# One decoder step on one core: an MLP seam without GpSimd, other PSUM banks for two transposes per head pair, and decode transposes later

## The chip, the cores and the metric

The kernel runs on one core of one Trainium2 chip. The metric is the device time of one execution in microseconds, the median of several runs. The core has a TensorE (PE) for matmuls, VectorE (DVE), ScalarE (ACT) and GpSimd (POOL) for elementwise work, SyncE (SP), which here only issues DMAs, and 16 DMA engines. Each engine works through its own instruction list in order and waits on semaphores of the others. Matmul results land in PSUM, which the kernel uses as eight banks; everything else lives in SBUF.

## The reference

One layer of a hybrid decoder, for 512 new tokens of one sequence (prompt) and one new token for each of 8 sequences with a window of 2048 cached rows (sample). All numbers are fp32.

```python
D_MODEL = 2048; SEQ = 512; DEC_BATCH = 8; DEC_SEQ = 1; PAST_LEN = 4096
HEAD_DIM = 64; N_HEADS = 16; D_FF = 4 * D_MODEL; D_IN = 3 * 1024 + 3 * 1024
DILATED_CONFIGS = ((128, 1), (512, 4), (2048, 16))

def reference(...):
        q, k, v, u, gb = _mixer_inputs(xp, norm_mix[l], w_in[l], q_norm[l], k_norm[l])
        o = _combine_branches([_dilated_branch_prompt(q, k, v, bias_c, d)
                               for bias_c, (_, d) in zip(biases, DILATED_CONFIGS)])
        ...
        yc = _depthwise_conv(ucat, conv_w[l], s_p)
        xp = xp + _mixer_output(o, yc, gb, attn_out_norm[l], conv_out_norm[l], w_out[l])
        xp = xp + _mlp(xp, norm_mlp[l], w_up[l], w_down[l])
        ...
        q, k, v, u, gb = _mixer_inputs(xs, norm_mix[l], w_in[l], q_norm[l], k_norm[l])
        kcat = jnp.concatenate([state_attn_k[l].astype(k.dtype), k], axis=1)
        ...
        ks_new.append(kcat[:, t_s:t_s + wb])      # the state shifted by one row
        vs_new.append(vcat[:, t_s:t_s + wb])

def _mlp(x, g, w_up, w_down):
    h = _rmsnorm(x, g)
    a = jnp.square(jax.nn.relu(jnp.einsum('bsd,df->bsf', h, w_up)))
    return jnp.einsum('bsf,fd->bsd', a, w_down)
```

The outputs are both token streams, the new keys and values of the prompt, and for the samples the key and value states of 8 x 2048 rows shifted by one row, which is a copy of some 131 MB from memory to memory (read and written).

## The kernel before

**Matmuls in three passes.** An fp32 operand is split into a high part `whi` (a rounded copy, on ScalarE) and a low part `wlo` (the rest, a subtraction on VectorE; L148/L149 for projections, L787/L788 in the MLP). A product is then three passes: high by high, high by low, low by high, on tiles of 128 rows by 260 columns (512 prompt and 8 sample tokens make two such halves). A weight tile of 512 KB is loaded by SyncE, split, and used by one product.

**Attention stage** (to about 420 us). `proj` runs the projections of q, k and v for eight head pairs j = 0..7 through `block` (L213). Inside a product, `step` is called after every third matmul and lets a generator advance: `norm_gen` (the RMS norm of q and k, its matmul on L408) and `attn_gen` (the attention of a pair). A `yield from wait(n)` means n such steps, so 3n matmuls. The order of instructions on each engine is fixed by the order in which this code emits them. `attn_gen` emits for each pair: scores of four row blocks into the `pS` banks (two heads, two banks), their softmax, then transposes. `trans(hp, tb)` (L475) transposes the normalized weights of head `hp` and row block `tb` on TensorE (L479), and evicts them as a high part on ScalarE (L482) and a low part on VectorE (L483). `pv(hp)` (L485) multiplies them by the values into a `pS` bank (L489). For a pair the order is trans(0,0) to trans(0,2) among the scores, trans(0,3), `pv(0)`, trans(1,0) to trans(1,3), `pv(1)`. PSUM is handed out in turn: `wtile` (L204) gives one of two `pw` banks, `stile` (L207) one of two `pS` banks. An instruction that writes a bank waits until the bank's previous readers are done.

**Decode stage** (about 420 to 690 us). The conv projections run on TensorE, and `dec_gen` (L561) advances beside them in the same way. It computes the 8 samples' attention: VectorE multiplies keys by queries, the scores are transposed, normalized (L635, L636), transposed again on L641, and the values of each batch b = 0..7 are multiplied, added (L664, L669) and summed with a matmul on L674. Batch b's wait ahead of L674 is 10 steps.

**MLP** (about 860 to 2166 us). 64 groups of seven products each (Winograd's form of a 2 x 2 block product, product number n = 7 gi + pi): groups 0 to 31 are the up half, groups 32 to 63 the down half in eight chunks c of four. A product is 24 matmuls of L1030, and after two of three of them `step` is called. `q_prep(n)` loads the four weight quarters of the next group (`q_load`, tiles `rg` and `raw`), splits the operand of product n + 2, and does one of the four sums of quarters that Winograd's form needs (`q_sum`, L848): sum 1 of the next group at pi = 3, sum 2 at pi = 5, sum 3 at pi = 0, sum 4 at pi = 1. Two things are special. In groups below `ADDED` = 4, sum 1 is done by a DMA that GpSimd issues and that adds the fourth quarter to the second while it loads (L826, L828). And `on_vector(gi, i)` (L837) gives sums 2 and 4 of group 31 and sums 1, 2 and 4 of group 32 to GpSimd instead of VectorE.

At the seam (groups 30 to 32) the down half's operands of chunk 0 must be ready: `op_gen(0)` loads and splits seven operands (`put`, L1001: two ScalarE and two VectorE instructions on L787/L788, tile `R`), one in each product of group 31.

**State shift.** `copy_chunk` (L135) issues one of 368 copies of 356 KB from SyncE. In the MLP two of three products issue one (L1100).

Of the kernel before, what the change touches and what calls it, by code (L numbers as in the profile page):

```python
# [33 lines left out]
NB = 8  # L34
# [50 lines left out]
def hymba_kernel(ctx, tc, xT, wi, wo, wu, wd, state_k, state_v, sconv, relb, relrep, ohp, lcp, ohd, lcd,  # L85
# [111 lines left out]
    def wait(n):  # L197
        for _ in range(n):
            yield
# [4 lines left out]
    def wtile():  # L204
        return p2.tile([128, 512], F32, name="pw", bufs=2)

    def stile():  # L207
        return p2.tile([128, 512], F32, name="pS", bufs=2)
# [216 lines left out]
    def attn_gen(j):  # L425
        while done.get(("norm", j)) != 2:
            yield
        if j not in TB:
            load_T(j)
        yield from wait(1 if j else 10)  # L430
        st = wtile()
        for i in range(3):
            T.transpose(st[:NB, i * 128:(i + 1) * 128], flat(RAW[i, j])[:, SEQ:], ident)
        yield from wait(3)
        stg = wt((NB, 3, 128), name="stg")
        S.activation(stg.rearrange("p a b -> p (a b)"), st[:NB, :384], AF.Copy)
        SP.dma_start(scr_qkv[:, :, j * 128:(j + 1) * 128], stg)
        st = wtile()
        for s in range(4):
            T.transpose(st[:, s * 128:(s + 1) * 128], flat(RAW[2, j])[:, s * 128:(s + 1) * 128], ident)  # L440
        yield from wait(3)
        sv = st.rearrange("p (s h e) -> p h s e", s=4, h=2)
        S.activation(vv[:, :, :, 0], sv, AF.Copy)
        V.tensor_tensor(vv[:, :, :, 1], sv, vv[:, :, :, 0].bitcast(F32), OP.subtract)
        yield
        pt = {}

        def products(tb):

            w = (tb + 1) * 128  # L450
            q = slice(tb * 128, (tb + 1) * 128)
            ss = [stile() for _ in range(2)]
            for n, (a, b) in enumerate(((qh, kh), (qh, kl), (ql, kh))):
                for hp in range(2):
                    r = slice(hp * E, (hp + 1) * E)
                    T.matmul(ss[hp][:, :w], a[r, q], b[r, :w], start=n == 0, stop=n == 2)
            return ss

        def score(hp, tb, s):
            w = (tb + 1) * 128  # L460
            lg = late(j, tb) if hp else wt((128, 512), name="lg")
            sm = wk.tile([128, 4], F32, name="sm", bufs=8)
            V.tensor_tensor_reduce(out=lg[:, :w], in0=s[:, :w], in1=TB[j][:, hp, 512 - w:], scale=1.0, scalar=-3e38,
                                   op0=OP.add, op1=OP.max, accum_out=sm[:, 0:1])
            V.tensor_scalar(sm[:, 1:2], sm[:, 0:1], -1.0, None, op0=OP.mult)
            S.activation(lg[:, :w], lg[:, :w], AF.Exp, bias=sm[:, 1:2], accum_out=sm[:, 2:3])
            pt[hp, tb] = lg, sm

        def norm_p(hp, tb):
            w = (tb + 1) * 128  # L470
            lg, sm = pt[hp, tb]
            V.reciprocal(sm[:, 3:4], sm[:, 2:3])
            V.tensor_scalar(lg[:, :w], lg[:, :w], sm[:, 3:4], None, op0=OP.mult)

        def trans(hp, tb):  # L475
            lg, sm = pt.pop((hp, tb))
            st = wtile()
            for s in range(tb + 1):
                T.transpose(st[:, s * 128:(s + 1) * 128], lg[:, s * 128:(s + 1) * 128], ident)  # L479
            sv = st.rearrange("p (s t) -> p s t", s=4)[:, :tb + 1]  # L480
            q = slice(tb * 128, (tb + 1) * 128)
            S.activation(pth[:, :tb + 1, q], sv, AF.Copy)  # L482
            V.tensor_tensor(ptl[:, :tb + 1, q], sv, pth[:, :tb + 1, q].bitcast(F32), OP.subtract)  # L483

        def pv(hp):  # L485
            st = stile()
            for s in range(4):
                for n, b in enumerate((pth, ptl)):
                    T.matmul(st[:, s * 128:], vv[:, hp, s].rearrange("p c e -> p (c e)"), b[:, s, s * 128:],  # L489
                             start=s == 0 and n == 0, stop=s == 3 and n == 1, skip_group_check=True)  # L490
                yield
            r = slice(hp * E, (hp + 1) * E)
            o = flat(R3[:, j])[r, :SEQ]
            S.activation(o, st[:E, :], AF.Copy)
            V.tensor_tensor(o, st[E:, :], o, OP.add)
            yield

        for tb in range(4):
            ss = products(tb)
            for hp in range(2):  # L500
                score(hp, tb, ss[hp])
            yield from wait(4)
            if tb == 3:
                done["scores"] = j + 1
            for hp in range(2):
                norm_p(hp, tb)
            yield from wait(4)
            if tb:
                trans(0, tb - 1)
            yield from wait(3)  # L510
        if j < 6:
            toeplitz(j + 2)
        trans(0, 3)
        yield from wait(5)
        yield from pv(0)
        for tb in range(4):
            trans(1, tb)
            yield from wait(4)
        yield from wait(2)
        yield from pv(1)  # L520
# [40 lines left out]
    def dec_gen():  # L561
# [72 lines left out]
        yield from wait(2)  # L634
        V.reciprocal(sm[:, 3:4], sm[:, 2:3])  # L635
        V.tensor_scalar(lg, lg, sm[:, 3:4], None, op0=OP.mult)  # L636
        yield from wait(2)
        yield from wait(2)
        st = wtile()
        for g in range(3):  # L640
            T.transpose(st[:NP[g], g * 128:(g + 1) * 128], lg[:, GOFF[g]:GOFF[g] + NP[g]], ident)  # L641
# [17 lines left out]
        for n in range(len(items) + 1):  # L659
            if n < len(items):  # L660
                b, g = items[n]
                t = tiles["v", b, g]
                w = pT[:NP[g], g, b * H:(b + 1) * H]
                V.tensor_tensor(t[:NP[g]], t[:NP[g]], w[:, :, None].to_broadcast([NP[g], H, E]), OP.mult)  # L664
            yield from wait(6)
            if n and items[n - 1][1]:
                b, g = items[n - 1]
                a = tiles["v", b, 0]
                V.tensor_tensor(a[:NP[g]], a[:NP[g]], tiles.pop(("v", b, g))[:NP[g]], OP.add)  # L669
                if g == 2:  # L670
                    a = tiles.pop(("v", b, 0)).rearrange("p h e -> p (h e)")
                    yield from wait(10)
                    for c in range(4):
                        T.matmul(od[32 * c:32 * c + 32, :256], sel[:, 31 - b:63 - b], a[:, 256 * c:256 * c + 256],  # L674
                                 start=b == 0, stop=b == NB - 1, skip_group_check=True)
                    prev(n + 2)
            prev(n + 2)
            yield from wait(3)
# [121 lines left out]
                                          for o in range(2) for h in range(2)}))  # L800
    NG = len(groups)
    Q = {}
    ADDED = 4

    def q_load(gi, o, h):
        if gi >= NG:
            return
        src = groups[gi][3][o, h]
        if o == 0:
            t = sl.tile([128, 8, 128], F32, name="raw", bufs=3)  # L810
            Q[gi, o, h] = t
            SP.dma_start(t, src)
        elif gi < 2:
            Q[gi, o, h] = [wt((128, 4, 128), name="rw") for _ in range(2)]
            for i in range(2):
                SP.dma_start(Q[gi, o, h][i], src[:, 4 * i:4 * i + 4])
        else:
            t = gt([128, 8, 128], name="rg")
            Q[gi, o, h] = t
            SP.dma_start(t, src)  # L820
        if (o, h) == (1, 0) and gi < ADDED:

            a22 = groups[gi][3][1, 1]
            if gi < 2:
                for i in range(2):
                    P.dma_start(Q[gi, o, h][i], a22[:, 4 * i:4 * i + 4], accum_op=OP.add)  # L826
            else:
                P.dma_start(t, a22, accum_op=OP.add)  # L828
# [5 lines left out]
        else:  # L834
            yield qs

    def on_vector(gi, i):  # L837

        if gi < 31:
            return True  # L840
        return i in {31: (1, 3), 32: (3,)}.get(gi, (1, 2, 3, 4))

    def q_sum(gi, i):
        out, a, b, op = SUMS[i]
        if gi < NG and not (i == 1 and gi < ADDED):
            e = V if on_vector(gi, i) else P
            for o_, a_, b_ in pieces(Q[gi, *out], Q[gi, *a], Q[gi, *b]):
                e.tensor_tensor(o_, a_, b_, op)  # L848

    SUMS = {1: ((1, 0), (1, 0), (1, 1), OP.add),  # L850
            2: ((0, 0), (1, 0), (0, 0), OP.subtract),
# [233 lines left out]
    for n in range(7 * NG):  # L1085
# [11 lines left out]
            C_ = pa.tile([128, 2, 512], F32, name=nm[pa], bufs=2)  # L1097
        ps = {0: A_, 1: None if pi < 1 else D_, 3: None if pi < 3 else C_}[{0: 0, 1: 1, 2: 0, 3: 3, 4: 0, 5: 1, 6: 0}[pi]]
        q_prep(n)
        if n % 3 != 2:  # L1100
            copy_chunk()
        product(n, ps, op_view(XO[OPS[pi]] if kind == "up" else DO[c, OPS[pi]]), 8 if kind == "up" else 4)

# [62 lines left out]
        if kind == "up" and gi == 31:  # L1166
# [3 lines left out]
                free_slots.extend(dslots[2 * pi - 4:2 * pi - 2])  # L1170
            if pi == 0:
                gens[0] = op_gen(0)
            next(gens[0])
        elif kind == "down":
            if g == 3:
                free_slots.append(DO.pop((c, OPS[pi])))
            if c == 0 and (g, pi) in ((0, 0), (1, 0)):
                free_slots.append([[wk.tile([128, 2, HT], F32R, name="wo", tag="w", bufs=16)
                                    for _ in range(2)] for _ in range(2)])
# [81 lines left out]
```

## Time and profile before

| | us |
|---|---|
| median of 3 runs | 2166.95 (2166.39 to 2168.46) |
| the profiled execution | 2167.66 |
| its span, first to last instruction | 2166.0 |
| TensorE busy | 2134.5 (99%) |
| VectorE busy | 1766.3 (82%) |
| ScalarE busy | 957.9 (44%) |
| GpSimd busy | 68.5 (3%) |
| DMA | 459.83 MB in 137935 packets |

Busy times come from one profiled execution. A matmul's length in the profile overlaps the next one's, so TensorE counts as busy as long as matmuls follow each other without a pause. Where it is not busy, the profile names the instruction on another engine whose end released it. All times in the text count from the span's start.

### The profile page before, as it was taken

How to read it: one execution, taken by the hardware profiler on the slowest of the kernel's cores; microseconds unless marked ns; L12 is line 12 of the kernel's file. 1: busy time of each engine (PE TensorE's matmuls, PEld its weight loads, DVE VectorE, ACT ScalarE, POOL GpSimd, SP SyncE). 2: the span in 40 equal slices, each digit the busy share in tenths (PEclk: the TensorE clock that was granted, in tenths of full speed). 3: DMA queues.
4: the chain of work that ended last, by engine and by line, in shares of the span. 5: the costliest groups of instructions: out<-in, count | busy, mean ns of one | idle time of the engine just before them, and what ended most of it. 6: DMA issues, size and time to landing. Idle time of an engine off the chain costs nothing.

```text
span 2166.0 us, 42326 instructions
## 1 busy us (share of the span) xinstructions
PE 2134.5 (99%) x17594; PEld 2105.7 (97%) x17594; DVE 1766.3 (82%) x2421; ACT 957.9 (44%) x1379; POOL 68.5 (3%) x83
## 2 busy tenths in 40 slices
PE   8999999999999999999999999999999999999999
PEld 8888999999999999999999999999999999999999
DVE  7777776698786657798888888888999999999997
ACT  5444444321223235554444444445444444444443
POOL 1001010000000000000000000002000000000000
PEclk9999999999999999999999999999999999999999
DMA  5344543476464647666776676677876666666653
GB/s 208 124 165 148 169 161 113 139 229 210 153 186 155 245 155 243 226 221 241 253 236 219 245 246 215 246 253 269 314 291 250 225 226 251 231 224 246 239 200 122
DMA packets 137935, 459.83 MB, mean 212 GB/s; under 512 B 19504, under 2 KB 49840, under 8 KB 131344
## 3 DMA queue, kind: packets, MB, share of 16 engines
q1 hardware_dynamic: 136320, 454.81, 60.4%
q0 software_dynamic: 864, 2.10, 0.5%
q8 instruction: 138, 2.26, 0.4%
q14 instruction: 53, 0.43, 0.1%
q10 hardware_dynamic: 560, 0.22, 0.0%
HBM read 414.31 MB, written 181.16 MB: 275 GB/s over the span
## 4 chain that ended last, share of the span: by engine, by line
PE 63%; DVE 4%; ACT 1%; issue 1%; DMA 1%; DVEq 0%; SPq 0%
PE mn L1030 29%; PE mm L1030 29%; PE mm L213 5%; DVE R L788 1%; DVE wlo L149 1%; DVE wlo L788 1%; DVE x1t L934 0%; DVE acc L927 0%; DMA ra<-scr_a 0%; ACT sq L925 0%; ACT whi L148 0%; ACT x L936 0%; ACT R L936 0%; ACT R L787 0%; DMA ovs<-state_v 0%
## 5 line engine op out<-in xcount | busy, mean ns | idle before, releaser
L213 PE MATMUL mm<-R,whi 128*128 128x260 f32 x4000 | 677.7, 287 | 5.7 <-ACT whi L148 5.6
L213 PEld LDWEIGHTS mm<-R,whi 128*128 128x128 f32 x4000 | 560.8, 189 | 19.0 <-issue 8.6
L1030 PE MATMUL mm<-R,whi 128*128 128x260 f32 x3008 | 547.7, 283 | 1.7 <-ACT cs L1113 1.2
L1030 PE MATMUL mn<-R,whi 128*128 128x260 f32 x3008 | 547.5, 283 | 0.0
L1030 PEld LDWEIGHTS mm<-R,whi 128*128 128x128 f32 x3008 | 463.3, 188 | 2.1 <-ACT cs L1113 1.4
L1030 PEld LDWEIGHTS mn<-R,whi 128*128 128x128 f32 x3008 | 463.3, 188 | 0.1
L1030 PE MATMUL mn<-R,wlo 128*128 128x260 f32 x1504 | 425.0, 283 | 2.4 <-DVE wlo L788 2.4
L1030 PE MATMUL mm<-R,wlo 128*128 128x260 f32 x1504 | 425.1, 283 | 1.3 <-DVE wlo L788 1.3
L213 PE MATMUL mm<-R,wlo 128*128 128x260 f32 x2000 | 404.0, 284 | 0.0
L788 DVE TENSOR_TENSOR wlo<-raw,whi 128x1024 fp32r<-128x1024 f32 x255 | 311.9, 1223 | 109.3 <-ACT whi L787 107.5
L787 ACT ACTIVATE whi<-raw 128x1024 fp32r<-128x1024 f32 x255 | 269.3, 1056 | 207.4 <-PE mn L1030 95.3
L213 PEld LDWEIGHTS mm<-R,wlo 128*128 128x128 f32 x2000 | 310.0, 189 | 0.4
L787 ACT ACTIVATE whi<-rg 128x1024 fp32r<-128x1024 f32 x186 | 197.3, 1061 | 215.9 <-PE mn L1030 91.5
L1030 PEld LDWEIGHTS mn<-R,wlo 128*128 128x128 f32 x1504 | 283.2, 188 | 3.0 <-DVE wlo L788 3.0
L1030 PEld LDWEIGHTS mm<-R,wlo 128*128 128x128 f32 x1504 | 283.2, 188 | 1.8 <-DVE wlo L788 1.7
L788 DVE TENSOR_TENSOR wlo<-rg,whi 128x1024 fp32r<-128x1024 f32 x186 | 228.1, 1226 | 1.5 <-ACT whi L787 1.4
L148 ACT ACTIVATE whi<-raw 128x1024 fp32r<-128x1024 f32 (+1 forms) x129 | 133.7, 1038 | 167.5 <-PE mm L213 134.0
L149 DVE TENSOR_TENSOR wlo<-raw,whi 128x1024 fp32r<-128x1024 f32 (+1 forms) x129 | 155.5, 1206 | 45.6 <-ACT whi L148 43.6
L848 DVE TENSOR_TENSOR raw<-raw 128x1024 f32<-128x1024 f32 x62 | 75.6, 1219 | 0.0
L848 DVE TENSOR_TENSOR rg<-rg,raw 128x1024 f32<-128x1024 f32 x62 | 75.5, 1218 | 0.0
L848 DVE TENSOR_TENSOR raw<-rg,raw 128x1024 f32<-128x1024 f32 x60 | 73.5, 1225 | 2.1
L1150 DVE TENSOR_TENSOR yacc<-mm,yacc 128x520 f32<-128x520 f32 x96 | 66.6, 694 | 7.3 <-PE mm L1030 6.3
(227 smaller groups left out, 2291.2 us busy)
## 6 DMA issues: line engine op xcount, KB each, us to landing
oks<-state_k SPq DMA_DIRECT2D x184, 356.0 KB
ovs<-state_v SPq DMA_DIRECT2D x184, 356.0 KB
raw<-wi SPq DMA_DIRECT2D x94, 512.0 KB
raw<-wu SPq DMA_DIRECT2D x64, 512.0 KB
rg<-wd SPq DMA_DIRECT2D x64, 512.0 KB
raw<-wd SPq DMA_DIRECT2D x64, 512.0 KB
rg<-wu SPq DMA_DIRECT2D x60, 512.0 KB
raw<-wo SPq DMA_DIRECT2D x32, 512.0 KB
```

Of the source, the lines that this page charges most:

```text
L148: S.activation(his[i][:, h], raws[i][:, h], AF.Copy)
L149: V.tensor_tensor(los[i][:, h], raws[i][:, h], his[i][:, h].bitcast(F32), OP.subtract)
L213: T.matmul(ps[t][:, :HT] if isinstance(ps, tuple) else ps[:, t, :HT], a[:, k, :], b[:, t, :], start=start and n == 0, stop=stop and n == 2)
L787: S.activation(hi, src, AF.Copy)
L788: eng.tensor_tensor(lo, src, hi.bitcast(F32), OP.subtract)
L848: e.tensor_tensor(o_, a_, b_, op)
L1030: T.matmul(ps[:, r, :HT], a[:, k, :], b(kt), start=n % 7 in ((0, 1, 3) if kts == 8 else (0, 1)) and kt == 0 and m == 0, stop=kt == kts - 1 ...
L1150: V.tensor_tensor(dst[:, r], v[:, r], dst[:, r], OP.add)
```

## The change

Five edits. Line numbers behind them differ by up to seven.

- In `trans`, blocks (0,3) and (1,0) of each pair take a bank with `stile` (`pS`) and not with `wtile` (`pw`).
- In `dec_gen`, the transposes of the normalized scores come 9 steps after the normalization, where it was 4, and the last batch waits 14 steps ahead of L674, where it was 10.
- `on_vector` is gone: no Winograd sum runs on GpSimd. Sum 1 of groups 31, 32 and 33 is done by the accumulating load that groups 0 to 3 have; the other sums of these groups run on VectorE.
- `copy_chunk` is not called in groups 30 to 32, and is called in every product of groups 4 to 10.
- `op_gen(0)` advances at pi = 0, 2, 4, 6 of group 31 and pi = 0, 2, 3 of group 32, where it was every product of group 31.

```diff
         def trans(hp, tb):
             lg, sm = pt.pop((hp, tb))
-            st = wtile()
+
+            st = stile() if (hp, tb) in ((0, 3), (1, 0)) else wtile()
...
         V.tensor_scalar(lg, lg, sm[:, 3:4], None, op0=OP.mult)
-        yield from wait(2)
-        yield from wait(2)
+        yield from wait(9)
         st = wtile()
...
-                    yield from wait(10)
+                    yield from wait(10 if b < NB - 1 else 14)
...
-    ADDED = 4
+    ADDED = (0, 1, 2, 3, 31, 32, 33)
...
-        if (o, h) == (1, 0) and gi < ADDED:
+        if (o, h) == (1, 0) and gi in ADDED:
...
-    def on_vector(gi, i):
-
-        if gi < 31:
-            return True
-        return i in {31: (1, 3), 32: (3,)}.get(gi, (1, 2, 3, 4))
-
     def q_sum(gi, i):
         out, a, b, op = SUMS[i]
-        if gi < NG and not (i == 1 and gi < ADDED):
-            e = V if on_vector(gi, i) else P
+        if gi < NG and not (i == 1 and gi in ADDED):
             for o_, a_, b_ in pieces(Q[gi, *out], Q[gi, *a], Q[gi, *b]):
-                e.tensor_tensor(o_, a_, b_, op)
+                V.tensor_tensor(o_, a_, b_, op)
...
-        if n % 3 != 2:
+        if not 30 <= gi <= 32 and (n % 3 != 2 or 4 <= gi <= 10):
             copy_chunk()
...
-            next(gens[0])
+            if pi % 2 == 0:
+                next(gens[0])
...
+            if gi == 32 and pi in (0, 2, 3):
+                next(gens[0])
```

TensorE's order in pair 0, around transposes (0,3) and `pv(0)`, before (`mm` is a projection's bank, `ident` the identity that a transpose multiplies by):

```order
L213 MATMUL mm<-R_76,whi 128x260 x3
L408 MATMUL pw<-sq,bd 128x260 x2
L479 MATMUL pw<-ident,lg 128x128 x4
L213 MATMUL mm<-R_76,whi 128x260
L213 MATMUL mm<-R_76,wlo 128x260 x2
L213 MATMUL mm<-R_76,whi 128x260 x4
L213 MATMUL mm<-R_76,wlo 128x260 x2
```

The same place after the change:

```order
L213 MATMUL mm<-R_76,whi 128x260 x3
L408 MATMUL pw<-sq,bd 128x260 x2
L480 MATMUL pS<-ident,lg 128x128 x4
L213 MATMUL mm<-R_76,whi 128x260
L213 MATMUL mm<-R_76,wlo 128x260 x2
L213 MATMUL mm<-R_76,whi 128x260 x4
L213 MATMUL mm<-R_76,wlo 128x260 x2
```

No instruction has moved; the four transposes write another bank.

VectorE's order at the seam before, from the end of group 30 into group 31 (`R` is an operand split of `put`, `wlo` a weight split, `cs` an eviction):

```order
L788 TENSOR_TENSOR wlo<-raw,whi 128x1024
L848 TENSOR_TENSOR rg<-rg,raw 128x1024
L788 TENSOR_TENSOR R_76<-ra,R_76 128x520 x2
L788 TENSOR_TENSOR wlo<-raw,whi 128x1024
L788 TENSOR_TENSOR R_76<-ra,R_76 128x520 x2
L788 TENSOR_TENSOR wlo<-rg,whi 128x1024
L788 TENSOR_TENSOR R_76<-ra,R_76 128x520 x2
L788 TENSOR_TENSOR wlo<-raw,whi 128x1024
L1115 TENSOR_TENSOR cs<-mn,cs 128x260
L788 TENSOR_TENSOR R_76<-ra,R_76 128x520 x2
L788 TENSOR_TENSOR wlo<-rg,whi 128x1024
L1117 TENSOR_TENSOR cs<-mn,cs 128x260
```

The same place after the change (L841 is the sum that was L848, L1108, L1110 and L1112 the evictions that were L1115, L1117 and L1119):

```order
L788 TENSOR_TENSOR wlo<-raw,whi 128x1024
L841 TENSOR_TENSOR rg<-rg,raw 128x1024
L788 TENSOR_TENSOR R_76<-ra,R_76 128x520 x2
L788 TENSOR_TENSOR wlo<-raw,whi 128x1024
L841 TENSOR_TENSOR raw<-raw 128x1024
L788 TENSOR_TENSOR wlo<-rg,whi 128x1024
L788 TENSOR_TENSOR R_76<-ra,R_76 128x520 x2
L788 TENSOR_TENSOR wlo<-raw,whi 128x1024
L1108 TENSOR_TENSOR cs<-mn,cs 128x260
L788 TENSOR_TENSOR wlo<-rg,whi 128x1024
L1110 TENSOR_TENSOR cs<-mn,cs 128x260
L788 TENSOR_TENSOR R_76<-ra,R_76 128x520 x2
```

Every second pair of `R` splits has moved back, and sum 4 of group 31, which GpSimd did, stands where one of them was.

GpSimd's last instructions before, from its accumulating loads on:

```order
L826 DMA rw<-wu 128x512 x4
L828 DMA rg<-wu 128x1024 x2
L848 TENSOR_TENSOR raw<-rg,raw 128x1024
L848 TENSOR_TENSOR raw<-raw 128x1024
L848 TENSOR_TENSOR rg<-rg 128x1024
L848 TENSOR_TENSOR raw<-rg,raw 128x1024
L848 TENSOR_TENSOR raw<-raw 128x1024
```

And after the change:

```order
L715 COPY cs_o<-up 128x8
L826 DMA rw<-wu 128x512 x4
L828 DMA rg<-wu 128x1024 x3
L828 DMA rg<-wd 128x1024 x2
L1248 UNCONDITIONAL_BRANCH
```

The five sums are gone, and three accumulating loads of groups 31 to 33 have come.

## Rows read from the trace of the kernel before

**Rows 1.** Windows by stage: busy us per engine, granted clock, DMA share, GB/s.

```profile
core 0: us, PE busy (x) PEld busy (x) DVE busy (x) ACT busy (x) POOL busy (x), PEclk, DMA share, GB/s
...
860.00:900.00 40.00, 36.18 (x295) 35.31 (x294) 35.31 (x52) 25.77 (x44) 2.62 (x3) 1.00 0.80 262
900.00:1480.00 580.00, 580.00 (x4833) 579.88 (x4831) 485.68 (x581) 278.25 (x380) 0.86 (x1) 1.00 0.68 233
...
1500.00:1532.00 32.00, 28.68 (x230) 27.66 (x229) 31.97 (x34) 17.86 (x26) 9.06 (x3) 1.00 1.00 370
...
1550.00:1600.00 50.00, 50.00 (x419) 50.00 (x418) 48.36 (x57) 23.06 (x25) 0.00 (x0) 1.00 0.93 351
```

**Rows 2.** TensorE's waits, whole span: us in total, times, longest.

```profile
PE pw L479 <- DVE R L483: 9.1, 11, 1.3
...
PE pw L674 <- DVE kv L669: 1.0, 1, 1.0
PE pw L641 <- DVE lg L636: 0.9, 1, 0.9
```

**Rows 3.** TensorE's waits from 1450 to 1560 us, the seam.

```profile
PE mn L1030 <- DVE wlo L788: 1.7, 2, 1.5
PE mm L1030 <- DVE wlo L788: 0.9, 1, 0.9
PE mm L1030 <- DVE yacc L1150: 0.5, 1, 0.5
PE mn L1030 <- ACT R L787: 0.2, 1, 0.2
```

**Rows 4.** The page's costliest groups: busy us, mean ns of one, idle before.

```profile
L1030 PE MATMUL mm<-R,whi 128*128 128x260 f32 x3008 | 547.7, 283 | 1.7 <-ACT cs L1113 1.2
```

**Rows 5.** Timeline of VectorE in pair 1: start, us, instruction.

```profile
131.91 0.55 DVE L483 TENSOR_TENSOR R<-pw,R 128x384 fp32r<-128x384 f32 x1
132.37 1.21 DVE L149 TENSOR_TENSOR wlo<-raw,whi 128x1024 fp32r<-128x1024 f32 x1
```

**Rows 6.** Timeline of TensorE, pairs 0 and 1: start, us, instruction, idle before.

```profile
87.82 0.66 PE L479 MATMUL pw<-ident,lg 128*128 128x128 f32 x4 [1.16 <-DVE R L483]
...
90.12 0.62 PE L489 MATMUL pS<-R 128*128 128x512 f32 x2
...
130.84 0.50 PE L408 MATMUL pw<-sq,bd 128*128 128x260 f32 x2 [0.86 <-DVE h L414]
132.51 1.10 PE L479 MATMUL pw<-ident,lg 128*128 128x128 f32 x4 [1.16 <-DVE R L483]
...
136.36 0.63 PE L489 MATMUL pS<-R 128*128 128x512 f32 x2
...
146.06 0.65 PE L479 MATMUL pw<-ident,lg 128*128 128x128 f32 x4 [0.81 <-DVE R L483]
```

**Rows 7.** A window in pair 1, columns as in rows 1.

```profile
133.00:134.00 1.00, 1.00 (x6) 1.00 (x5) 0.59 (x1) 0.35 (x1) 0.00 (x0) 0.50 0.00 0
```

**Rows 8.** Timeline of GpSimd at the seam, three of its five sums.

```profile
1488.60 2.43 POOL L848 TENSOR_TENSOR raw<-rg,raw 128x1024 f32<-128x1024 f32 x1 [586.33 <-DVE wlo L788]
...
1502.28 3.41 POOL L848 TENSOR_TENSOR rg<-rg 128x1024 f32<-128x1024 f32 x1 [2.88 <-DMA rg<-wd]
...
1523.06 3.25 POOL L848 TENSOR_TENSOR raw<-raw 128x1024 f32<-128x1024 f32 x1 [7.15 <-DVE rg L848]
```

**Rows 9.** Timeline of VectorE at the seam.

```profile
1489.66 1.93 DVE L1130 SCALAR_TENSOR_TENSOR cs<-cs,rstd 128x520 f32<-128x520 f32 x1
...
1492.99 0.69 DVE L1130 SCALAR_TENSOR_TENSOR cs<-cs,rstd 128x520 f32<-128x520 f32 x1
...
1495.11 1.22 DVE L848 TENSOR_TENSOR rg<-rg,raw 128x1024 f32<-128x1024 f32 x1
...
1513.31 0.41 DVE L1119 TENSOR_TENSOR cs<-mm,cs 128x260 f32<-128x260 f32 x1
...
1524.59 2.81 DVE L788 TENSOR_TENSOR wlo<-rg,whi 128x1024 fp32r<-128x1024 f32 x1
```

**Rows 10.** Line 828, the accumulating loads of groups 2 and 3.

```profile
DMA to landing us min/median/max: 6.4/7.5/8.7
```

## The prediction

> **What bounds the kernel now.** I read the stages first, then what TensorE waits for, then the lines around each wait. In most of the program TensorE is never idle: in groups 2 to 29 of the MLP it is busy 580.00 of 580 us [rows 1], so nothing outside TensorE's own idle time can be won. The list of its waits over the whole span shows where that idle time is: 9.1 us in 11 waits of the transposes on line 479, each for VectorE's L483, and one wait each of 0.9 and 1.0 us in the decode stage, at L641 and L674 [rows 2]. The list for 1450 to 1560 us adds the MLP seam, where the up products end and the down products begin: 1.7 + 0.9 + 0.5 + 0.2 = 3.3 us in five waits [rows 3]. There VectorE is the bound: 31.97 us busy in 32, with TensorE at 28.68 [rows 1].
>
> A wait costs a little more than the idle time listed. A 260-column matmul is modelled 283 ns long [rows 4], but matmuls follow each other every 580.00/4833 = 0.120 us [rows 1], so each wait also loses 0.283 - 0.120 = 0.16 us of overlap. I add 0.16 per removed wait.
>
> **Attention: two transposes on score banks.** The waits on L479 come from the bank, not from the data. Before transposes (0,3) of pair j = 1, L483 reads the previous result out of a bank at 131.91 for 0.55 us, so until 132.46 [rows 5]; the transposes start at 132.51, after 1.16 us of idle time [rows 6]. There are two `pw` banks, the norm's L408 takes one of them in between, and so the transposes need the bank that L483 has not yet emptied. In the change, transposes (0,3) and (1,0) go to the `pS` banks, which are free there: the scores of the pair are long evicted, and `pv(0)` takes the other one. The order of work on TensorE is the same; only the bank differs. With (1,0) out of the `pw` turn, (1,1) and (1,2) also find a bank whose last reader is long done. One of the 11 waits stays, (1,3) of pair 1 at 146.06 with 0.81 us [rows 6], because (1,2) and (1,3) still share a turn. So 9.1 - 0.81 = 8.3 us in ten waits, plus 10 x 0.16, is 9.9 us. L408's wait of 0.86 us [rows 6] is for L414, which the change does not touch; I leave it.
>
> There is more at pair 1. From the start of transposes (0,3) to the start of `pv(0)` the same instructions take 90.12 - 87.82 = 2.30 us in pair 0 and 136.36 - 132.51 = 3.85 us in pair 1 [rows 6]. [...]
>
> One new wait is to be paid. With (0,3) of pair 1 starting 1.3 us earlier, `pv(0)` is due at 132.51 - 1.32 + 2.30 = 133.49, but the low part of its operand (L483) stands on VectorE behind the L149 that ends at 132.37 + 1.21 = 133.58 [rows 5]; 0.69 us of L483 behind that puts the second matmul of `pv(0)` about 0.5 us late. Attention: 9.9 + 1.55 - 0.5 = **10.9 us**. Bounds: 6 if half of the waits return at the next bank, 11.5 if the new wait does not come.
>
> **Decode.** L641's transposes move 5 steps later; a step is three matmuls, so 15 x 0.12 = 1.8 us against the 0.9 us they waited. The last batch's L674 moves 4 further steps, 1.44 us against 1.0. Both waits go: 0.9 + 1.0 + 2 x 0.16 = 2.2 us. The whole V phase moves 5 steps later against the projections, whose VectorE work keeps its place. So the additions L669 of batches 0 and 2 land behind other VectorE instructions, the largest of which is a split of 1.21 us like L149 [rows 5]. By the order a wait of about 0.3 us appears at each; bounds 0 and 1.2 each. Nothing else is queued behind on TensorE but projections. The key and value loads that SyncE issues from these steps pass one or two weight loads, which have whole products of lead; the phase still ends before the projections do. I cost that at nothing, and at up to 1 us if the lead were gone. Decode: 2.2 - 0.6 = **1.6 us** (0.5 to 2.2).
>
> **The seam.** Before, GpSimd does five of the Winograd sums between 1488.60 and 1526.3, 2.4 to 3.4 us each [rows 8]. Beside each one a VectorE instruction is stretched: L1130 takes 1.93 us at 1489.66 and 0.69 at 1492.99; the last of five is a split at 1524.59 with 2.81 instead of 1.21 [rows 9]. Together the five lose 9.3 us. With GpSimd idle this is gone. VectorE gets four of the five sums at 1.22 us each [rows 9] and loses two that it had, as sum 1 of groups 31, 32 and 33 becomes an accumulating load: +2.4 us. Three of seven operand splits move from group 31 into group 32; each is two VectorE instructions on 128x520 tiles like L1130 at 0.69 us [rows 9], so 4.1 us of work moves to where its due times are later. Net: VectorE has 6.9 us less to do in a stretch in which TensorE lost 3.3 + 5 x 0.16 = 4.1 us to it. By the new order it stays within 0.1 to 1 us of each due time, so I leave 0.4 us of waits. Seam: **3.7 us**, bounds 4.1 and -2 (lower if a sum stands in front of a split that is due).
>
> The accumulating loads must land before sum 2 reads them, or VectorE stops in order, with the splits behind it, and TensorE behind those. In the first seam two such loads landed 6.4 to 8.7 us after their issue [rows 10]. For group 32, both plain loads had landed by 1502.28, when GpSimd's third sum started [rows 8]; the first of the two, which is all that the accumulate needs, is issued ahead, and without the copies in the queue it should be there by about 1499. Then 1499 + 7.5 to 8.7 is 1506.5 to 1508; sum 2 is now in the row ahead of the eviction that ran at 1513.31 in the slowed order of before [rows 9], and TensorE had lost some 2 us by then. That is 2 to 4 us of room; the other groups have about the same. I cost the loads at nothing; without that room each microsecond of lateness is one of VectorE.
>
> [...]
>
> The copies: 16 more in groups 4 to 10 and 14 fewer in groups 30 to 32. The DMA share is 0.68 in 900 to 1480 [rows 1]; a 356 KB copy occupies the engines for about 1 us, so 16 of them in seven groups of 20 us are 16/141 = 0.11 more, some 0.8. At a share of 0.93, TensorE is still busy 50.00 us of 50 [rows 1]. Cost: nothing; at most 16 x 1 us if every copy delayed a weight load that was due.
>
> **Sum.** 10.9 + 1.6 + 3.7 = 16.2 us. The profiled execution took 2167.66 us, its span 2166.0; 2167.66 - 16.2 = 2151.5. The median of the runs is 0.7 us lower, so 2150.8; I say 2151.
>
> **Rivals.** First, VectorE keeps the clock of attention: the removed waits come back at the next instruction that needs it, as at `pv(0)` of pair 1. For it: the remaining waits on L414 and L483 [rows 6]. Against it: most pairs have only one or two short waits, with matmuls of a projection between. If half returns, attention gives 5.5 and not 10.9: 2156.5.
>
> Second, the clock falls in pair 1 all the same, since the wait of 0.86 us stays: 1.55 us less, 2152.5.
>
> Third, the slower side: the accumulating loads starve at the seam. VectorE has about 6.9 - 4.1 = 2.8 us to spare there, so a total lateness of L costs L - 2.8. With landing 12 us after issue each load is about 2.5 us late, 7.5 in all: 4.7 lost, 2155.7. To end slower than before by over 0.2%, L must be 16.2 + 4.3 + 2.8 = 23 us, about 7.8 per load, so landing some 17.5 us after issue, twice the longest row [rows 10]; at 20 us it would be 2151 + 31.5 - 2.8 = 2180.
>
> Fourth, the denser copies saturate the queues in groups 4 to 10: by their own length at most 16 us, which ends at about 2167, no change.
>
> Fifth, the change does not do what it says: the transposes wait at the `pS` banks as they did at `pw`. Then only decode and seam are left: 2166.95 - 5.3 = 2161.6.
>
> **How the numbers follow.** Forecast 0.68 (2147 to 2154, the low end if the waits at 130.84 and 146.06 shrink too); first rival 0.10; second 0.07; third 0.07, of which 0.03 slower; fourth 0.05, of which 0.02 faster, 0.02 no change and 0.01 slower; fifth 0.03, at the edge of no change. A measurement of this kernel tells about 0.2%, 4.3 us, from no change. Faster: 0.68 + 0.10 + 0.07 + 0.04 + 0.02 = 0.91; the same 0.05; slower 0.04. The range of 2147.5 to 2159 takes in the forecast, the first two rivals and the milder side of the third.
>
> **What would show it.** Right: no wait on the transposes' line but one of 0.8 us near 140 us; granted clock 1.00 throughout attention; no wait at the decode transposes; L1130 and the splits at the seam at 0.69 and 1.21 us, TensorE busy 31.5 of 32 us there; the new loads landing within 9 us. Wrong: waits on L483 moved to `pv`, a long VectorE wait on a DMA in groups 31 to 33, or TensorE waiting for splits in groups 4 to 10.

## The result and the profile after

The changed kernel takes 2150.82 us (median of 4 runs, 2150.38 to 2151.33) beside 2167.16 us for the kernel before (4 runs, 2166.39 to 2168.46): a ratio of 0.9924, with a 95% interval from 0.9912 to 0.9936. The prediction was 2151.0. Its profiled execution took 2150.38 us with a span of 2148.4.

TensorE's waits over the whole span of the changed kernel (us in total, times, longest us; L480 is the transposes' line, L479 before, and L490 the weighted sum, L489 before), against [rows 2]:

```profile
PE pw L408 <- DVE h L414: 1.5, 3, 0.9
...
PE pw L480 <- DVE R L484: 0.8, 1, 0.8
...
PE pS L490 <- DVE R L484: 0.7, 2, 0.4
...
PE pw L674 <- DVE kv L669: 0.3, 1, 0.3
```

Of 9.1 us in 11 waits of the transposes one of 0.8 us is left; L641 is gone from the list, and L674 keeps 0.3 of 1.0 us. From 1450 to 1560 us, against [rows 3]:

```profile
PE mn L1023 <- DVE yacc L1143: 0.2, 1, 0.2
```

Windows of the changed kernel, columns as in [rows 1]:

```profile
900.00:1480.00 580.00, 580.00 (x4833) 579.88 (x4832) 485.85 (x584) 278.23 (x381) 0.86 (x1) 1.00 0.71 244
1486.70:1514.00 27.30, 27.30 (x230) 27.30 (x228) 25.64 (x33) 18.61 (x27) 1.73 (x2) 1.00 0.95 321
1500.00:1532.00 32.00, 31.81 (x264) 31.54 (x263) 31.45 (x41) 18.98 (x24) 0.86 (x1) 1.00 0.80 265
```

TensorE is as dense as before in groups 2 to 29 although the DMA share rose from 0.68 to 0.71. At the seam it is busy 31.81 us of 32 from 1500 to 1532 us, where it was 28.68. That window holds later work now, since the changed kernel is 13 to 18 us ahead there. The matmuls that ran from 1500 to 1532 us before now run from about 1486.7 to 1514.0, in 27.3 us without a pause, and VectorE is busy 25.64 us beside them, where it was 31.97: it has 6.3 us less to do for the same matmuls. Its rows at the L1123 (L1130 before) that took 1.93 us in [rows 9], at sum 2 of group 32, which GpSimd did before, and at sum 2 of group 33; both sums read an accumulating load:

```profile
1476.80 0.70 DVE L1123 SCALAR_TENSOR_TENSOR cs<-cs,rstd 128x520 f32<-128x520 f32 x1
...
1495.95 1.22 DVE L841 TENSOR_TENSOR raw<-rg,raw 128x1024 f32<-128x1024 f32 x1
...
1517.13 1.23 DVE L841 TENSOR_TENSOR raw<-rg,raw 128x1024 f32<-128x1024 f32 x1
```

To see where the time went, I took the start of the same matmul in both timelines: the first of L408 (48 us), the last weighted sum of attention (419 us), the first of the MLP (861 us), one ahead of the seam's first wait (1497.64 us, product 2 of group 31), one behind its last (1551.28 us, late in group 33), and the last. The lead over the profiled execution before, taken from one such matmul to the next, is the gain of that stretch. "Start" is the lead at the first L408, which lies up to 0.8 us off the kernel before with no difference in the code there.

| kernel | start | attention | decode | MLP up to the seam | seam | rest | all |
|---|---|---|---|---|---|---|---|
| changed kernel | 0.47 | 11.15 | 1.69 | 0.03 | 4.05 | 0.12 | 17.51 |
| the same, second time (e11_after) | 0.48 | 10.79 | 1.69 | -0.01 | 4.01 | 0.15 | 17.11 |
| e1_banks | -0.41 | 11.28 | -0.01 | 0.05 | 0.01 | -0.01 | 10.91 |
| e2_decode | -0.71 | 0.36 | 1.70 | 0.07 | 0.00 | -0.01 | 1.41 |
| e3_seam | 0.27 | 0.66 | -0.01 | 0.08 | 3.77 | 0.16 | 4.93 |
| e4_pair1 | -0.09 | 10.70 | 1.70 | 0.03 | 4.06 | 0.15 | 16.55 |
| e5_copies | -0.69 | 11.24 | 1.69 | 0.04 | 0.77 | -0.83 | 12.22 |
| e6_splits | -0.02 | 10.96 | 1.69 | -0.01 | 1.90 | 0.18 | 14.70 |
| e7_sum1 | -0.20 | 11.46 | 1.69 | -0.01 | 2.92 | 0.15 | 16.01 |
| e8_gpsimd | -0.26 | 11.14 | 1.71 | 0.01 | 2.37 | 0.15 | 15.12 |
| e9_bank13 | -0.77 | 12.77 | 1.69 | 0.00 | 4.06 | 0.15 | 17.90 |
| e10_copies_sum1 | -0.05 | 11.47 | 1.70 | 0.03 | 2.91 | -0.83 | 15.23 |
| e12_both | -0.39 | 12.46 | 1.69 | 0.00 | 3.98 | 0.02 | 17.76 |

### The profile page after: what moved, and what is told of

Read it like the earlier page. It is cut to its first block, busy times and chain, and to the rows that moved or that the text cites. A ratio compares the mean times of both kernels' runs of the same rounds, so it can differ in the third digit from the quotient of the medians.

```text
span 2148.4 us, 42322 instructions
## 1 busy us (share of the span) xinstructions
PE 2129.5 (99%) x17594; PEld 2103.1 (98%) x17594; DVE 1758.7 (82%) x2423; ACT 957.8 (45%) x1379; POOL 56.6 (3%) x81
## 4 chain that ended last, share of the span: by engine, by line
PE 89%; DVE 6%; ACT 2%; DMA 2%; issue 1%; SPq 0%; DVEq 0%; ACTq 0%
PE mn L1023 30%; PE mm L1023 29%; PE mm L213 26%; DMA raw<-wi 2%; DVE wlo L149 1%; PE pS L456 1%; PE pS L490 1%; DVE R L788 1%; PE pw L480 1%; ACT whi L148 1%; DVE x1t L927 0%; DVE acc L920 0%; DVE wlo L788 0%; ACT sq L918 0%; DVE kv L664 0%
## 5 line engine op out<-in xcount | busy, mean ns | idle before, releaser
L841 DVE TENSOR_TENSOR raw<-raw 128x1024 f32<-128x1024 f32 x64 | 78.0, 1218 | 0.0
L841 DVE TENSOR_TENSOR raw<-rg,raw 128x1024 f32<-128x1024 f32 x62 | 76.0, 1225 | 2.1
L841 DVE TENSOR_TENSOR rg<-rg,raw 128x1024 f32<-128x1024 f32 x62 | 75.5, 1218 | 0.0
L1143 DVE TENSOR_TENSOR yacc<-mm,yacc 128x520 f32<-128x520 f32 x96 | 66.6, 694 | 7.0 <-PE mm L1023 6.0
```

Source lines behind the costliest of these rows:

```text
L841: V.tensor_tensor(o_, a_, b_, op)
L1143: V.tensor_tensor(dst[:, r], v[:, r], dst[:, r], OP.add)
```

## The experiments

### Each part alone: e1_banks, e2_decode, e3_seam

The edits are those of the diff, one group at a time: the line with `stile` in e1_banks; the two `wait` edits in e2_decode; all the others in e3_seam.

> The kernel before with the bank edit alone: transposes (0,3) and (1,0) of each pair on score banks. Theory (the ten waits come from the bank, and the clock drop of pair 1 hangs on one of them): 10.9 us faster than before, so about 2156.2, one wait of 0.8 us left on the transposes, granted clock 1.00 from 125 to 140 us, the decode waits of 0.9 and 1.0 us and the seam's 3.3 us unchanged. Rival (VectorE keeps the clock of attention, and part of the gain in the changed kernel belongs to other edits): 5 to 6 us faster, about 2161.5, with new waits on L414 or on the low parts ahead of the weighted sums.

Measured: 2156.90 us, ratio 0.9949 (0.9937 to 0.9962); 11.28 us in attention and nothing elsewhere. One wait of 0.8 us is left on the transposes, the granted clock is 1.00 throughout, and decode and seam wait as before. The theory holds; VectorE does not give the waits back.

> The kernel before with the decode edit alone: 9 steps ahead of the transposes, 14 ahead of the last batch's sum. Theory: 2.2 us of waits go and 0.3 to 0.6 us come back at the sums of batches 0 and 2, so 1.6 us faster, about 2165.5. Rival (what moves 5 steps later meets weight loads or VectorE work it did not meet, and gives it all back): no change, 2167.2, with as much waiting at L674 as was removed.

Measured: 2165.83 us, ratio 0.9990 (0.9981 to 0.9998); 1.70 us in the decode stage, with one listed wait of 0.3 us left at the batches' sums. The theory holds.

> The kernel before with the MLP edits alone: no sum on GpSimd, accumulating loads in groups 31 to 33, copies paused at the seam and denser in groups 4 to 10, operand splits spread over two groups; attention and decode as before. Theory: 3.7 to 4.2 us faster than before, about 2163.2; the three parts add up to the whole, 16.3 us. Rival (the parts lean on each other, because an earlier attention stage also moves the copies and the loads of the MLP against the compute): under 2 or over 6 us, and the three parts do not add up.

Measured: 2162.60 us, ratio 0.9978 (0.9968 to 0.9987); 3.77 us at the seam, as the theory has it. By stage the parts add up: 11.28, 1.70 and 3.77 alone, 11.15, 1.69 and 4.05 together. By medians, 11.2 + 2.2 + 5.5 = 18.9 us against the 2168.06 of the kernel before beside them are more than the 16 to 17 us of the whole; the next experiment shows why medians of the kernel before are a poor ruler.

### The clock in pair 1: e4_pair1

```diff
-            st = stile() if (hp, tb) in ((0, 3), (1, 0)) else wtile()
+            st = stile() if (hp, tb) in ((0, 3), (1, 0)) and (j, hp) != (1, 0) else wtile()
```

> The changed kernel, with transposes (0,3) of pair 1 alone back on the banks they had. Theory (the clock drop of pair 1 follows from the two waits there, 0.86 and 1.16 us): the wait of 1.16 us is back, 1.3 us, and with it a stretch of granted clock 0.50 of about 3.4 us, another 1.55 us, less the 0.6 us that the weighted sum of pair 1 now waits: 2.3 us slower than the changed kernel, about 2153.1. Rival (the drop had another cause, such as where in its own time the chip looked): only 0.7 us slower, 2151.5, and no granted clock under 1.00 from 120 to 140 us.

Measured: 2152.80 us, median of 5 runs from 2151.32 to 2152.95. Both answers were right, in different runs: two runs with a mean granted clock of 1.000 took 2151.32 and 2151.97 us, three with 0.999 took 2152.80, 2152.93 and 2152.95. The profiled execution is one of the first kind. TensorE's timeline there:

```profile
128.57 0.50 PE L408 MATMUL pw<-sq,bd 128*128 128x260 f32 x2 [0.86 <-DVE h L414]
130.24 0.66 PE L480 MATMUL pw<-ident,lg 128*128 128x128 f32 x4 [1.17 <-DVE R L484]
...
132.53 0.63 PE L490 MATMUL pS<-R 128*128 128x512 f32 x2
```

The two waits are back as in [rows 6], and yet the stretch from the transposes to the weighted sum takes 132.53 - 130.24 = 2.29 us, as in pair 0, at a granted clock of 1.00 from 128 to 133 us. The profiled execution of e3_seam, which has the banks of before, shows the same in pair 1 (134.96 - 132.67 = 2.29 us, granted clock 1.00 from 133 to 134 us), and the drop in pair 2 instead, again behind two waits, TensorE's timeline and a window:

```profile
174.77 0.51 PE L408 MATMUL pw<-sq,bd 128*128 128x260 f32 x2 [0.45 <-DVE h L414]
176.44 1.07 PE L480 MATMUL pw<-ident,lg 128*128 128x128 f32 x4 [1.16 <-DVE R L484]
...
177.00:178.00 1.00, 1.00 (x7) 1.00 (x6) 0.00 (x0) 0.46 (x1) 0.00 (x0) 0.50 1.25 520
```

So the drop lies behind two waits in these executions, and the same waits of pair 1 stand without it in two others. Of the 19 runs of the kernel before beside these four kernels, 13 have a mean granted clock under 1.000 and a median of 2168.2 us, and six have 1.000 and a median of 2166.4 us. All 41 runs of the changed kernel and of the kernels that have its banks in pair 1 have 1.000, e5_copies apart, which is told of below. By these medians the drop costs about 2168.2 - 2166.4 = 1.8 us when it comes, and with the banks it came in none of these runs.

### What carries the seam: e5_copies to e8_gpsimd

Each takes one edit back from the changed kernel, so its price is read from the seam's column against 4.05 us. Such a price is that of one execution, so the medians stand beside it: the changed kernel's are 2150.82 and, in e11_after, 2151.08 us.

```diff
-        if not 30 <= gi <= 32 and (n % 3 != 2 or 4 <= gi <= 10):
+        if n % 3 != 2:
```

> The changed kernel with the state shift as before: a copy in two of three products throughout, none more in groups 4 to 10, none fewer in groups 30 to 32. Theory (the seam's waits came from VectorE instructions that GpSimd stretched, and the pause of the copies is no part of the gain): within 0.5 us of the changed kernel, 2150.5 to 2151.5, no wait for splits from group 31 to 33, the accumulating loads landing at most 3 us later than the 6.1 to 9.4 us of the changed kernel. Rival (it is the DMA share of 1.00 at the seam that made it slow, and the pause is what pays): 2 to 4 us slower, 2153 to 2155, with VectorE or ScalarE waiting for loads in groups 31 to 33.

Measured: 2155.07 us, ratio 0.9944 (0.9929 to 0.9959); 3.3 us of the seam's 4.05 are gone, the most of all four. The theory failed; the rival was nearly right on the size (2153 to 2155), and the trace gives the path. GpSimd's issue of the accumulating load of group 33, the DMA with its us to landing, VectorE's sum 2, TensorE's next wait, and a window behind it, in e5_copies:

```profile
1509.99 0.86 POOL L828 DMA_DIRECT2D rg<-wd  x1 [21.56 <-DMA rg<-wd]
...
rg<-wd POOLq DMA_DIRECT2D x1, 512.0 KB, 9.9
...
1519.96 1.23 DVE L841 TENSOR_TENSOR raw<-rg,raw 128x1024 f32<-128x1024 f32 x1 [1.78 <-DMA rg<-wd]
...
1533.76 0.48 PE L1023 MATMUL mn<-R,whi 128*128 128x260 f32 x2 [1.92 <-DVE yacc L1143]
...
1535.00:1536.00 1.00, 1.00 (x7) 1.00 (x6) 1.00 (x2) 0.00 (x0) 0.00 (x0) 0.50 0.84 297
```

And GpSimd and the load's landing in the changed kernel:

```profile
1507.35 0.86 POOL L828 DMA_DIRECT2D rg<-wd  x1 [19.57 <-DMA rg<-wd]
...
rg<-wd POOLq DMA_DIRECT2D x1, 512.0 KB, 9.4
```

In both, GpSimd waits for the plain load of the same tile before it may add to it. With the copies in the queue that load comes later: VectorE reaches sum 2 at 1516.95 + 1.23 = 1518.18, 8.2 us behind the issue, where in the changed kernel it is 1517.13 - 1507.35 = 9.8 us. The load takes 9.9 against 9.4 us. So 0.4 us of room became 1.8 us of waiting. VectorE, which is full there (busy 15.00 us of 15 from 1520 to 1535), carries it for 14 us to the eviction that TensorE waits for, 1.92 us, and behind that one wait the granted clock is 0.87 from 1534 to 1535 us, 0.50 from 1535 to 1538 and 0.93 from 1538 to 1539. Two of four runs have a mean clock of 0.999 (2155.68 and 2156.09) and two 1.000 (2154.24 and 2154.46). The profiled execution is 2155.68, so its 3.3 us hold the drop, which is worth 1.5 us between the two pairs of runs; without it the pause of the copies is worth about 1.8 us at the seam. Another 0.95 us is lost behind it (0.83 us in place of a gain of 0.12), of which e10_copies_sum1 tells below.

```diff
-            if pi % 2 == 0:
-                next(gens[0])
+            next(gens[0])
-            if gi == 32 and pi in (0, 2, 3):
-                next(gens[0])
```

> The changed kernel with all seven operand splits of the down half in group 31 again. Theory (VectorE has only about a microsecond of room at each due time there, so 3.7 us of splits in front of due work must show): 1 to 2.5 us slower than the changed kernel, about 2152.5, TensorE waiting for weight splits in group 31, with the waits before group 32 over. Rival (without GpSimd VectorE has room enough in group 31): no change, 2150.8.

Measured: 2151.62 us (2151.03 to 2153.09); 0.5 to 0.8 us above the changed kernel, under the forecast of 1 to 2.5. By stage it is 2.15 us slower at the seam, but the profiled execution, 2153.09, is the slowest of the four (the other three are 2151.03 to 2151.80), so that is the most that the places of the splits are worth. In that execution the cause is only half the one I gave. The waits in 1478 to 1502 us:

```profile
ACT R L787 <- DMA ra<-scr_a: 3.4, 2, 2.5
...
DVE R L788 <- ACT R L787: 1.9, 1, 1.9
...
PE mn L1023 <- DVE cs L1110: 1.2, 1, 1.2
```

ScalarE reaches the splits before their operands are loaded and stops for 3.4 us; VectorE has an idle 1.9 us behind it. It is not VectorE's load alone but the order: a split stands ahead of due work and waits for its own data. Spread over two groups, each split finds its operand there: the changed kernel lists no such wait. Whether the three faster runs have it too, no trace shows.

```diff
-    ADDED = (0, 1, 2, 3, 31, 32, 33)
+    ADDED = (0, 1, 2, 3)
```

> The changed kernel with sum 1 of groups 31, 32 and 33 on VectorE in place of the accumulating loads: three more VectorE instructions of 1.22 us, in groups 30, 31 and 32, and three loads back on SyncE. Theory: groups 31 and 32 are full on VectorE, and two of the three show: 1 to 2.4 us slower than the changed kernel, about 2152.5. Rival (the accumulating loads buy nothing, since VectorE had 29.45 us busy of 30 but no wait): within 0.4 us, 2150.5 to 2151.2.

Measured: 2151.93 us (2151.76 to 2152.17); 1.13 us at the seam, at the lower end of the theory, as one TensorE wait of 1.0 us for ScalarE's `whi`. So the accumulating loads do buy something, about one of the three sums that they save.

```diff
-                V.tensor_tensor(o_, a_, b_, op)
+                (P if (gi, i) in ((31, 2), (31, 4), (32, 2), (32, 4)) else V).tensor_tensor(o_, a_, b_, op)
```

> The changed kernel with sums 2 and 4 of groups 31 and 32 on GpSimd again, everything else as changed. Theory (a sum on GpSimd takes 2.4 to 3.4 us and stretches the VectorE instruction beside it by 1.2 to 2.2 us, more than the 1.22 us that it saves there): VectorE loses 4 x 1.9 - 4 x 1.22 = 2.7 us net in a full stretch, and each wait comes late, so 2 to 3.5 us slower than the changed kernel, about 2153.5, with stretched L788 and L1123 rows beside each GpSimd sum. Rival (the splits' new places and the paused copies carry the gain): within 0.5 us, 2150.5 to 2151.5.

Measured: 2152.20 us (2151.62 to 2152.62); 1.68 us at the seam, below the 2 to 3.5 of the theory and clear of the rival. Three of GpSimd's four sums, and VectorE's rows beside them:

```profile
1476.00 2.43 POOL L841 TENSOR_TENSOR raw<-rg,raw 128x1024 f32<-128x1024 f32 x1 [9.05 <-DMA raw<-wu]
...
1488.62 2.70 POOL L841 TENSOR_TENSOR raw<-raw 128x1024 f32<-128x1024 f32 x1
...
1497.91 2.40 POOL L841 TENSOR_TENSOR raw<-rg,raw 128x1024 f32<-128x1024 f32 x1 [6.60 <-DVE wlo L788]
...
1477.06 1.92 DVE L1123 SCALAR_TENSOR_TENSOR cs<-cs,rstd 128x520 f32<-128x520 f32 x1
...
1489.05 3.44 DVE L788 TENSOR_TENSOR R<-ra,R 128x520 fp32r<-128x520 f32 x2 [1.22 <-ACT R L787]
...
1498.21 2.66 DVE L1123 SCALAR_TENSOR_TENSOR cs<-cs,rstd 128x520 f32<-128x520 f32 x1
```

The stretching is as before (0.70 us becomes 1.92 and 2.66), and in the rows it goes with how long the sum still runs. The sums end at 1478.43 and 1500.31 us, the two L1123 rows at 1478.98 and 1500.87, so 0.55 us later each. In the kernel before it is the same: the sum ends at 1488.60 + 2.43 = 1491.03 ([rows 8]), L1130 at 1489.66 + 1.93 = 1491.59 ([rows 9]). All nine sums of the two kernels have one such instruction, which starts beside the sum, reads two tiles in SBUF and ends 0.55 to 1.1 us behind it. Evictions that read a PSUM bank keep their length beside a sum in these rows: L1119 at 1489.20 takes 0.43 us and L1150 at 1523.98 takes 0.69 in the kernel before (0.41 at 1513.31, 0.69 at 1527.32 with no sum), L1143 at 1510.13 takes 0.69 in e8_gpsimd (0.69 at 1508.39). The four stretched places lose 1.2, 2.1, 2.0 and 1.6 us, 6.9 in all; less the 4.9 us of the four sums that GpSimd does, that is 2.0 us for VectorE and not the 2.7 of the theory.

### Copies and loads together: e10_copies_sum1

The edits of e5_copies and e7_sum1 at once.

> The changed kernel with the copies as before and sum 1 of groups 31 to 33 on VectorE, so the two edits of e5_copies and e7_sum1 together. With the copies as before, VectorE waited 1.8 us for the accumulating load of group 33, TensorE then waited 1.9 us, and the granted clock fell. Theory (the copies cost time only by making the accumulating load late): without such loads the copies cost nothing, so about what sum 1 on VectorE costs, 2151.9 within 0.6 us, no wait on a DMA at the seam, no granted clock of 0.50 there. Rival (the copies at the seam delay the other loads too): 2154 or more, with VectorE or ScalarE waiting for plain loads.

Measured: 2153.21 us (2152.58 to 2153.91), over the 2152.5 of the theory and under the 2154 of the rival. At the seam the theory holds: 2.91 us of gain, the 2.92 of e7_sum1, no stop for a load of sums (VectorE waits 0.5 us for the load of an operand), granted clock 1.00. So with no accumulating load the copies cost nothing there. But behind group 33 both kernels with the copies of before lose 0.83 us, spread over many groups with no wait listed on TensorE, which the kernel before, with the same copies, does not lose. No run tells why; it stays open.

### The wait that is left: e9_bank13 and e12_both, beside e11_after

```diff
-            st = stile() if (hp, tb) in ((0, 3), (1, 0)) else wtile()
+            st = stile() if (hp, tb) in ((0, 3), (1, 0), (1, 3)) else wtile()
```

and, in e12_both, also

```diff
-            P.tensor_tensor(sq, raw, raw, OP.mult)
-            P.tensor_tensor(sl_, sq, sh.bitcast(F32), OP.subtract)
+            e = V if (t, j) == (1, 2) else P
+            e.tensor_tensor(sq, raw, raw, OP.mult)
+            e.tensor_tensor(sl_, sq, sh.bitcast(F32), OP.subtract)
```

> The changed kernel as it is, beside the others of this call: 2150.8 within 0.6 us, granted clock 1.00 in every run.

> The changed kernel with a third block, (1,3), on score banks. Theory (the wait of 0.8 us that is left at pair 1's transposes is for a bank too): it goes, 0.8 + 0.16 us, and up to half comes back at pv(1) of pair 1, whose low part follows later on VectorE: 0.5 to 1.0 us faster than the changed kernel, about 2150.1. Rival (it is VectorE that is late there, not the bank): the wait is found again at pv(1), no change.

> The kernel of e9_bank13 with the two squaring instructions of one projection (k of pair 2), which run on GpSimd beside pair 1's normalizations L473 (1.31 and 1.34 us there, 0.49 in pair 0), on VectorE. Theory (the wait of 0.86 us at L408 of pair 1 comes from L473 stretched by 1.67 us; VectorE takes 1.2 us for the two instructions itself): 0.3 to 0.5 us of that wait goes, so 0.2 to 0.5 us faster than e9_bank13, about 2149.8, and L473 at 0.5 us there. Rival (VectorE's own two instructions take all of it back): no change against e9_bank13.

Measured side by side: 2151.08 us (2150.56 to 2152.14) for the changed kernel, 2149.86 (2149.34 to 2150.56) for e9_bank13, 2149.30 (2148.95 to 2150.27) for e12_both, ratio to the kernel before 0.9917 (0.9904 to 0.9930). The last wait on the transposes goes and is not found again; e9_bank13 is 1.2 us faster than the changed kernel by the medians, a little over the forecast of 0.5 to 1.0, and the ranges of the runs just touch. For e12_both the row under test moved as forecast; VectorE's timeline there, below the row in the changed kernel:

```profile
125.03 1.31 DVE L473 TENSOR_SCALAR lg<-lg,sm 128x512 f32<-128x512 f32 x1
...
126.20 0.70 DVE L538 TENSOR_TENSOR tmp<-raw 128x520 f32<-128x520 f32 x1
127.01 0.70 DVE L539 TENSOR_TENSOR sq<-tmp,sq 128x520 fp32r<-128x520 f32 x1
...
127.82 0.49 DVE L473 TENSOR_SCALAR lg<-lg,sm 128x512 f32<-128x512 f32 x1
```

L473 takes 0.49 us and not 1.31, but the longest wait at L408 only falls from 0.9 to 0.7 us, and the 0.6 us by which its median lies below that of e9_bank13 is inside the spread of both. It beats both kernels of this case; its second edit is not shown to help.

## Why the prediction held, step by step

**Attention** was 10.9 us in the sum and is 11.15 (10.79 in e11_after). The bank was the cause: ten of eleven waits are gone, the one named stays with its 0.8 us, and the new wait at the weighted sum of pair 1, put at about 0.5 us, is there. TensorE's timeline of the changed kernel:

```profile
128.19 0.51 PE L408 MATMUL pw<-sq,bd 128*128 128x260 f32 x2 [0.86 <-DVE h L414]
128.54 0.60 PE L480 MATMUL pS<-ident,lg 128*128 128x128 f32 x4
...
130.77 0.39 PE L490 MATMUL pS<-R 128*128 128x512 f32 x1
131.59 0.50 PE L490 MATMUL pS<-R 128*128 128x512 f32 x1 [0.43 <-DVE R L484]
```

The transposes follow L408 at once, without the 1.16 us of [rows 6]. **The clock** is the weak term: the 1.55 us in the sum are what the stretch of pair 1 took beyond that of pair 0 in [rows 6], at the granted clock of 0.50 of [rows 7], and were read from one execution as if every execution had them. No run shows that the second wait brings the drop every time: e4_pair1 and e3_seam have that wait in pair 1, 1.17 us in each, at a granted clock of 1.00. What the runs show is a mean clock under 1.000 in three of five runs of e4_pair1 and 13 of 19 of the kernel before, so about two of three, and in none of the 41 runs with the new banks. So against the median the term was worth about what I put down only because that median has the drop too, which was luck. The second rival, a clock that falls all the same, is refuted by e1_banks: five of five runs at 1.000.

**Decode** was 1.6 and is 1.69. The two new waits at the sums of batches 0 and 2 were put at 0.3 us each; the trace has 0.28 and 0.09.

**The seam** was 3.7 and is 4.05, but the size came out right for a reason that was only part of the cause. I rested it on the 9.3 us by which GpSimd's sums stretched VectorE, and gave the pause of the copies no gain of its own, although the landing times that I worked out assumed it. VectorE's own saving was about right: 6.9 us net in the sum, and 6.3 us less for the matmuls of 1500 to 1532 us, most of that stretch. One edit taken back at a time, the profiled executions lose 1.7 us with GpSimd, 2.15 with the places of the splits, 1.1 without the accumulating loads and 3.3 without the pause of the copies, twice the gain together. Two of these are high: 1.5 of the 3.3 us is the clock drop, and the median of e6_splits lies only 0.5 to 0.8 us above the changed kernel. With 1.8 and 0.8 the sum is 5.4 us, still more than the 4.05, so the edits are not independent. For two of them the runs show how: the accumulating loads gain 1.1 us when the copies are paused (4.05 against 2.92), and with the copies as before they are worse than none (0.77 in e5_copies, some 2.3 without the clock drop, against 2.91 in e10_copies_sum1). The step that failed is the room of the accumulating loads. I had 2 to 4 us; in the changed kernel they land 1.0, 1.6 and 0.4 us before VectorE needs them (issues at 1465.76, 1486.91 and 1507.35, landing 8.4, 7.4 and 9.4 us later, sums at 1475.20, 1495.95 and 1517.13). One of the signs was missed with it, that the new loads land within 9 us. The third rival was thus much nearer than its 0.07.

What made it near is not a landing like the 12 us it was reckoned with. In the changed kernel VectorE was busy 18.34 of 20 us from 1485 to 1505 and the load issued at 1486.91 landed in 7.4 us, inside the 6.4 to 8.7 of [rows 10]; the longest landing in e5_copies is 9.9 us. What came late in e5_copies was above all the issue (8.2 us ahead of the time that VectorE reached sum 2, against 9.8), behind a plain load that came later with the copies in the queue (GpSimd waits 21.56 us for it, against 19.57).

**The copies in groups 4 to 10**, the fourth rival, cost nothing: from the first product to the seam the lead changes by 0.03 us, with a DMA share in these groups of 0.81 (933 to 1074 us) against 0.71 before (946 to 1087 us). **The first and fifth rivals** ended with e1_banks.

## What to carry to other kernels

A matmul that waits for an eviction may be waiting for its bank, not its data: look at what read the bank last, and whether another pool has a free one at that moment, before taking work off the evicting engine. When an edit has several parts that meet in one place, take each away from the finished version as well as trying it alone, since a part that looks worthless by itself (a pause in the copies) can be what keeps another in time. And read a granted clock over several runs before booking it: one profiled execution does not say whether a drop is always there.

## What was not expected of the hardware

- The clock drop comes in some executions of a fixed program and not in others: 13 of 19 runs of the kernel before have a mean granted clock under 1.000 and six have 1.000, with medians of 2168.2 and 2166.4 us. Behind the same two waits in pair 1 TensorE ran at 0.50 in one execution (the kernel before, 133 to 134 us) and at 1.00 in another (e4_pair1, 128 to 133 us). In the traces the drop lies in pair 1 (the kernel before, and e2_decode with 0.50 from 133 to 136 us) or in pair 2 (e3_seam, 0.50 from 177 to 179 us).
- It also stands behind one wait of 1.92 us in a stretch with no other listed wait: in e5_copies the granted clock is 0.50 from 1535 to 1538 us, and two of four runs have a mean of 0.999.
- In all nine sums on GpSimd in the kernel before and e8_gpsimd, the VectorE instruction that reads two tiles in SBUF and starts beside the sum ends 0.55 to 1.1 us behind it: 0.70 becomes 1.92 or 2.66 us. L473, with one tensor input, takes 1.31 us in the changed kernel beside a GpSimd operation of 1.06 us (125.01 us), and 0.49 in e12_both with none beside it.
- The accumulating loads of 512 KB issued from GpSimd land 6.1 to 9.9 us after their issue, with a DMA share from 0.68 (changed kernel, 860 to 900 us) to 1.05 (e5_copies, 1505 to 1520 us) around them.
